# In the first pair of heads, the first head's two small query groups are transposed on TensorE and not through DRAM

## The chip, the cores and the metric

The kernel runs on one core of a Trainium2 chip. The metric is the time of one execution on the device in microseconds (us), smaller being better. Five engines work side by side, each through its own queue in order: PE (TensorE: matmuls, and PEld for its weight loads), DVE (VectorE), ACT (ScalarE), POOL (GpSimd) and SP, which here issues every DMA.

## The reference, cut to what matters

One decoder layer on x (1024 x 1024, fp32): RMSNorm, an input projection into eight parts, three mixers (causal pooling, stick-breaking attention, attention into a memory), each gated, then an output projection and the residual. The change is in the stick-breaking attention, 8 heads of 64 channels:

```python
z = einsum('bqhd,bkhd->bhqk', qb, kb) * Dh**-0.5      # a block of 128 queries, keys up to its end
mask = s_idx[None, :] < t_idx[:, None]
log_1m_beta = where(mask, log_sigmoid(-z), 0.0)
cum = cumsum(log_1m_beta, axis=-1)
log_a = log_sigmoid(z) + cum[..., -1:] - cum
a = where(mask, exp(log_a), 0.0)
out = einsum('bhqk,bkhd->bqhd', a, vb)
```

## The kernel before, in words

**The attention.** The 8 heads are worked off in four pairs. The queries of a head form four groups j = 0 to 3 of 256 queries (two blocks of 128), which look at 256, 512, 768 and 1024 keys. So there are 32 groups in the order (pair, j, head); in the first pair group 0 is head 0 with j = 0, group 1 is head 1 with j = 0, group 2 is head 0 with j = 1, and so on to group 7. Each group is cut into chunks of 256 keys, j + 1 of them: chunk 0 belongs to group 0, chunk 1 to group 1, chunks 2 and 3 to group 2, 4 and 5 to group 3, 6 to 8 to group 4, 9 to 11 to group 5. A group's last chunk is 384 columns wide (its upper triangle is left out), every other one 512.

For each block, `qk` (L743) multiplies queries with keys on PE (L754, tiles `z`), takes a sigmoid of -z on ACT into a scratch tile `be` (L760), and a scan on DVE turns it into running products (`scan`, L769). The result has queries on partitions and keys along the row, and the product with the values (`av`, L830, matmuls in `a_v` at L611) wants keys on partitions. Two ways lead there, and `by_dma` (L740) says which one a group takes:

- through DRAM: DVE transposes 32 x 32 squares (`turn`, L772), four DMAs per block write them to a DRAM tile `zd` so that the squares themselves change places (`store`, L780), and per chunk one or two DMAs bring them back to a tile `al` (`rd`, L801 to L807). ACT rounds that to `ah` (L826) and POOL subtracts to leave the low part in `al` (L827).
- on PE: `hl` (L810) calls `a_t` (L587), which transposes 128 x 128 blocks on PE into PSUM (L593, tiles `ta`), rounds them on ACT to `ah` (L597) and subtracts on DVE into `al` (L598).

Either way `a_v` multiplies first with `ah` and then with `al`. Before, the second head of each pair goes through DRAM whole, the first head only for j < 2.

**The order.** All engines' orders are written out by hand in this part. `sb_slots` gives each chunk e a slot: in slot e the kernel issues the reads of chunk e + 3, does `hl` of chunk e + 1 and `av` of chunk e. The `qk` steps of the groups are spread over slots ahead of their chunks (L857 to L863): the pair of groups n, n + 1 must be done 6 slots ahead of chunk first[n] when group n goes through DRAM, 3 slots ahead when it doesn't. Slots with nothing in them take no time. `weave` (L216) puts the slots between the steps of the input projection that PE does anyhow (the `fill`: units `u_q`, `u_k`, `u_g` of 16 steps, three 512-column matmuls to a step), giving each slot that has steps the same share of PE's planned time:

```python
span = sum(s.pe for s in main) + sum(c for c, _ in fill[: len(fill) - keep])
total = sum(s.occ + s.pe for s in main)
...
at_ = max([span * gone / total] + [ready.get(k, 0.0) for k in s.needs])
while n < len(fill) and now < at_:
```

Work that follows later is queued with `soon(us, fn)`: it is written into its engine's order once so many planned us have gone by (the scan 1.0 after its `qk`, a `turn` 1.1 + 0.0022 L and a `store` 3.4 + 0.0038 L for a row of L keys). The first pair's slots run from -12 to 8 beside 56 fill steps: the whole of `u_q` and `u_k` of the second pair, the gate unit `u_g` of the second pair, and half of that of the third. The first step of a unit also issues the load of the next unit's raw weights (`load`, L152, into the one buffer `wr`), and its steps 7, 9, 11 and 13 round quarters of them on ACT (L277) and subtract on POOL (L278).

**Buffers.** `be` tiles come from a ring of four, and every fifth and sixth from `Y0` and `Y1`; `al` is a ring of four, `ah` of two, the PSUM tiles `z` and `tr` (for `ta`) of two each.

Of the kernel before, what the change touches and what calls it, by code (L numbers as in the profile page):

```python
# [27 lines left out]
def layer_kernel(  # L28
# [707 lines left out]
    def sb_slots():  # L736
        groups = [(p, j, h) for p in range(4) for j in range(NT // 2) for h in range(2)]
        chunks = [(n, b) for n, (p, j, h) in enumerate(groups) for b in range(j + 1)]
        first = [chunks.index((n, 0)) for n in range(len(groups))]
        by_dma = [h == 1 or j < 2 for _, j, h in groups]  # L740
        be, zd, wt, acc, stored, n_be = {}, {}, {}, {}, [], [0]

        def qk(n, i, c):  # L743
# [418 lines left out]
    def y_load():  # L1162
# [13 lines left out]
        )  # L1176
    )
    attn = sb_slots()
    weave(attn[0], fill_0)
    weave(attn[1], fill_1)  # L1180
# [227 lines left out]
```

## Time and profile before

| | us |
|---|---|
| median of 3 runs (lowest to highest) | 518.09 (516.09 to 518.65) |
| the profiled execution | 514.25 |
| its span, first to last instruction | 512.5 |
| PE busy / DVE busy in the span | 491.7 / 405.4 |
| first `z` of the first pair | 136.23 |
| first `z` of the second pair | 197.06 |

All times of rows are us from the start of that span. The profiled execution took 1.75 us more than its span, and it is 3.84 us below the median of the runs.

### The profile page before, as it was taken

The numbers are of one execution on the slowest core, as the hardware profiler recorded it, in microseconds if no ns is written. First come the engines' busy times: TensorE is split into PE (matmuls) and PEld (weight loads), VectorE is DVE, ScalarE is ACT, GpSimd is POOL, SyncE is SP. The second block draws the span as 40 slices with busy tenths as digits, with TensorE's granted clock in tenths as the row PEclk, the third lists the DMA queues.
The fourth block names the chain that finished last, engine by engine and source line by source line (L and its number), as shares of the span: only waits on it lengthen the run. The fifth ranks groups of instructions, "written<-read, shape, count | busy, mean of one in ns | idle before, by whom it ended". The sixth has DMA issues, their size and how long they took to land.

```text
span 512.5 us, 8041 instructions
## 1 busy us (share of the span) xinstructions
PE 491.7 (96%) x2508; PEld 409.6 (80%) x2508; DVE 405.4 (79%) x618; ACT 297.3 (58%) x672; POOL 261.1 (51%) x254
## 2 busy tenths in 40 slices
PE   7999999999999799999999999999979989999997
PEld 6778888887888578888888888888758768888886
DVE  4787777777479578699988859878899659999954
ACT  7978757678455465566766666664754439362400
POOL 4480345265133336267662865765758870044990
PEclk9999999999999999999999999999999989999999
DMA  8911111532636944579876786768654822504023
GB/s 297 361 41 42 41 43 41 115 84 70 148 72 125 197 110 105 134 148 229 148 153 159 142 191 143 146 152 172 141 105 158 287 86 82 175 31 159 8 104 143
DMA packets 174979, 67.73 MB, mean 132 GB/s; under 512 B 125894, under 2 KB 164056, under 8 KB 174936
## 3 DMA queue, kind: packets, MB, share of 16 engines
q1 hardware_dynamic: 174936, 67.21, 52.6%
q8 instruction: 20, 0.33, 0.3%
q14 instruction: 23, 0.19, 0.1%
HBM read 43.59 MB, written 19.40 MB: 123 GB/s over the span
## 4 chain that ended last, share of the span: by engine, by line
PE 67%; DVE 10%; DMA 7%; ACT 5%; issue 4%; SPq 3%; POOL 3%; DVEq 0%; ACTq 0%; POOLq 0%
PE u_q L254 6%; PE av L611 6%; PE u_k L254 4%; DMA al<-zd 4%; PE u_v L254 4%; PE z L754 3%; DVE be L769 3%; PE u_q L251 3%; PE oS L1288 3%; PE oS L1290 3%; PE oS L1289 3%; SPq L780 3%; PE u_pg L254 2%; PE u_g L254 2%; PE u_k L251 2%
## 5 line engine op out<-in xcount | busy, mean ns | idle before, releaser
L769 DVE TENSOR_TENSOR_SCAN be<-be,later 128x128 f32<-128x128 f32 (+3 forms) x64 | 103.3, 1615 | 23.3 <-ACT be L760 22.7
L827 POOL TENSOR_TENSOR al<-al,ah 128x512 fp32r<-128x512 f32 (+1 forms) x52 | 76.4, 1474 | 37.0 <-ACT ah L826 32.7
L760 ACT ACTIVATE be<-z 128x128 f32<-128x128 f32 (+3 forms) x96 | 46.8, 489 | 33.9 <-PE z L754 25.8
L826 ACT ACTIVATE ah<-al 128x512 fp32r<-128x512 f32 (+1 forms) x52 | 30.1, 580 | 23.2 <-DMA al<-zd 21.2
L611 PE MATMUL av<-al,V_v 128*128 128x256 f32 (+1 forms) x160 | 32.8, 287 | 10.4 <-POOL al L827 6.0
L611 PEld LDWEIGHTS av<-ah,V_v 128*128 128x128 f32 x160 | 29.3, 188 | 9.7 <-ACT ah L826 2.9
L611 PEld LDWEIGHTS av<-al,V_v 128*128 128x128 f32 x160 | 24.1, 188 | 12.9 <-POOL al L827 7.5
L772 DVE STREAM_TRANSPOSE be<-be 128x128 f32<-128x128 f32 (+7 forms) x48 | 32.8, 685 | 1.1
L611 PE MATMUL av<-ah,V_v 128*128 128x256 f32 (+1 forms) x160 | 30.4, 271 | 2.1 <-ACT ah L826 2.1
L703 POOL TENSOR_SCALAR pe_m<-pe_m,nb_m 128x256 f32<-128x256 f32 x16 | 16.8, 1049 | 28.2 <-DVE nb_m L700 24.4
L597 ACT ACTIVATE ah<-ta 128x512 fp32r<-128x512 f32 (+1 forms) x28 | 15.9, 567 | 19.5 <-PE ta L593 17.8
L251 PE MATMUL u_v<-hh,wh_v 128*128 128x512 f32 x64 | 26.4, 412 | 0.0
L630 ACT ACTIVATE avt<-av,ve_v 64x128 f32<-64x128 f32 x64 | 19.8, 357 | 11.3 <-PE av L611 10.5
L251 PE MATMUL u_g<-hh,wh_g 128*128 128x512 f32 x64 | 26.2, 410 | 0.0
L1288 PE MATMUL oS<-bs,hh 128*128 128x512 f32 (+1 forms) x68 | 25.9, 381 | 0.0
L251 PE MATMUL u_k<-hh,wh_k 128*128 128x512 f32 x64 | 25.9, 404 | 0.0
L692 ACT ACTIVATE pe_m<-z_m,nb_m,qsc 128x256 f32<-128x256 f32 x32 | 17.8, 561 | 13.9 <-DVE nb_m L688 12.9
L1290 PE MATMUL oS<-bs,hl 128*128 128x512 f32 (+1 forms) x68 | 25.8, 379 | 0.0
L1289 PE MATMUL oS<-bs,hh 128*128 128x512 f32 (+1 forms) x68 | 25.6, 376 | 0.0
L754 PE MATMUL z<-KA_k,qa_q 128*128 128x512 f32 (+3 forms) x96 | 25.3, 348 | 0.0
L254 PE MATMUL u_v<-hl,wh_v 128*128 128x512 f32 x64 | 25.3, 395 | 0.0
L254 PE MATMUL u_g<-hl,wh_g 128*128 128x512 f32 x64 | 25.3, 395 | 0.0
(323 smaller groups left out, 1547.6 us busy)
## 6 DMA issues: line engine op xcount, KB each, us to landing
al<-zd SPq DMA_DIRECT2D x28, 256.0 KB, 3.1
x<-in_x_dram SPq DMA_DIRECT2D x8, 512.0 KB, 6.4
al<-zd SPq DMA_DIRECT2D x24, 128.0 KB, 3.2
wr_q<-in_w_in_dram SPq DMA_DIRECT2D x4, 512.0 KB, 5.3
wr_k<-in_w_in_dram SPq DMA_DIRECT2D x4, 512.0 KB, 5.0
wr_v<-in_w_in_dram SPq DMA_DIRECT2D x4, 512.0 KB, 3.8
KA_k<-KA_k SPq DMA_DIRECT2D x8, 256.0 KB, 4.8
KB_k<-KB_k SPq DMA_DIRECT2D x8, 256.0 KB, 3.9
```

The lines of the kernel that those rows point to most:

```text
L251: nc.tensor.matmul(pt[:], wh[:, kc], hh[k][:, c], start=(k == 0), stop=False)
L254: nc.tensor.matmul(pt[:], w[:, kc], h[k][:, c], start=False, stop=(k == KD - 1 and n == 1))
L611: nc.tensor.matmul(av[:, 256 - bw : 256], vs[n], part[:, o : o + bw], start=(first and part is ah and n == 0), stop=(last and part is al a ...
L754: nc.tensor.matmul(zp[:, 0:w], q[h][:, tcol], k[h][:, m, s0 : s0 + w], start=(m == 0), stop=(m == 1))
L760: nc.scalar.activation(t[:, s0 : s0 + w], zp[:, 0:w], AF.Sigmoid, scale=-(HD**-0.5))
L769: nc.vector.tensor_tensor_scan(t[:, rev], t[:, rev], mask, 1.0, op0=ALU.mult, op1=ALU.max)
L772: nc.vector.transpose(t[:, 0:L], t[:, 0:L])
L826: nc.scalar.activation(hi[:, 0:w], f(lo[:, 0:w]), AF.Copy)
L827: nc.gpsimd.tensor_tensor(lo[:, 0:w], f(lo[:, 0:w]), f(hi[:, 0:w]), op=ALU.subtract)
L1288: nc.tensor.matmul(bk[:, c], xh[:, tcol], wh[:, c], start=(n == 0), stop=False)
L1289: nc.tensor.matmul(bk[:, c], xh[:, tcol], wl[:, c], start=False, stop=False)
L1290: nc.tensor.matmul(bk[:, c], xl[:, tcol], wh[:, c], start=False, stop=(n == 3))
```

## The change

One line: which groups go through DRAM. In the first pair the groups 0 and 2 (first head, j = 0 and 1; chunks 0, 2 and 3) now take the way over PE. The slots and the interleaving follow from `by_dma`, so they move too.

```diff
-        by_dma = [h == 1 or j < 2 for _, j, h in groups]
+        by_dma = [h == 1 or (j < 2 and p > 0) for p, j, h in groups]
```

## Rows read from the trace of the kernel before

**Rows 1.** The page's first part: busy us, share of span, instructions.
```profile
PE 491.7 (96%) x2508; PEld 409.6 (80%) x2508; DVE 405.4 (79%) x618; ACT 297.3 (58%) x672; POOL 261.1 (51%) x254
```

**Rows 2.** Busy by stretch: length, PE, PEld, DVE, ACT, POOL, granted clock, DMA share.
```profile
134.00:170.00 36.00, 36.00 (x170) 29.63 (x169) 25.96 (x34) 16.89 (x38) 9.95 (x11) 1.00 0.54 109
170.00:196.00 26.00, 21.60 (x110) 17.37 (x109) 17.73 (x19) 14.20 (x31) 9.92 (x9) 1.00 0.71 161
196.00:230.00 34.00, 34.00 (x186) 29.06 (x185) 27.88 (x36) 20.05 (x46) 18.43 (x16) 1.00 0.54 114
```

**Rows 3.** Waits between 170 and 196: us in total, times, longest.
```profile
PEld av L611 <- POOL al L827: 3.1, 4, 1.1
...
PEld av L611 <- ACT ah L826: 2.1, 1, 2.1
...
PEld av L611 <- DVE al L598: 0.7, 2, 0.4
```

**Rows 4.** Timeline of ACT, 171 to 178 (start, us, idle before and releaser).
```profile
171.53 0.63 ACT L826 ACTIVATE ah<-al 128x512 fp32r<-128x512 f32 x1 [3.24 <-DMA al<-zd]
...
172.68 0.59 ACT L413 ACTIVATE g_g<-u_g 128x512 f32<-128x512 f32 x1
175.99 0.42 ACT L277 ACTIVATE wh_g<-wr_g 128x256 fp32r<-128x256 f32 x1 [2.71 <-DMA wr_g<-in_w_in_dram]
...
177.39 0.51 ACT L826 ACTIVATE ah<-al 128x384 fp32r<-128x384 f32 x1
```

**Rows 5.** Timeline of SP's queue, 149 to 178.
```profile
149.31 9.59 SPq L780 DMA_DIRECT2D zd<-be  x16
...
168.90 0.85 SPq L152 DMA_DIRECT2D wr_g<-in_w_in_dram  x1
...
172.34 5.31 SPq L780 DMA_DIRECT2D zd<-be  x4
177.76 0.47 SPq L801 DMA_DIRECT2D al<-zd  x1
```

**Rows 6.** Timeline of PE: the first product of chunk 2 to the second pair's first z.
```profile
172.52 0.40 PE L611 MATMUL av<-ah,V_v 128*128 128x256 f32 x2
173.58 0.51 PE L611 MATMUL av<-al,V_v 128*128 128x256 f32 x2 [0.66 <-POOL al L827]
...
177.95 0.45 PE L611 MATMUL av<-ah,V_v 128*128 128x256 f32 x2 [1.65 <-ACT ah L826]
179.30 0.45 PE L611 MATMUL av<-al,V_v 128*128 128x256 f32 x2 [0.90 <-POOL al L827]
...
197.06 0.33 PE L754 MATMUL z<-KB_k,qb_q 128*128 128x128 f32 x2
```

**Rows 7.** The chain that ended last: a chunk's transposes, and issue steps beside them.
```profile
202.78 0.44 PE ta L593 x4
...
203.44 0.47 PE u_q L254 x2
...
211.89 0.33 PE ta L593 x3
...
212.92 0.47 PE z L754 x2
213.38 0.47 PE av L611 x4
```

**Rows 8.** Groups by line: busy us, mean ns of one.
```profile
L593 PE MATMUL ta<-ident,be 128*128 128x128 f32 x104 | 15.9, 272 | 0.0
```

**Rows 9.** DVE's groups by shape, 134 to 200: busy us, mean ns, idle before.
```profile
L769 DVE TENSOR_TENSOR_SCAN be<-be,later 128x896 f32<-128x896 f32 x2 | 4.7, 2352 | 4.1 <-ACT be L760 4.1
L769 DVE TENSOR_TENSOR_SCAN be<-be,later 128x768 f32<-128x768 f32 x2 | 4.1, 2036 | 3.0 <-ACT be L760 3.0
L769 DVE TENSOR_TENSOR_SCAN be<-be,later 128x640 f32<-128x640 f32 x2 | 3.4, 1682 | 1.0 <-ACT be L760 1.0
...
L772 DVE STREAM_TRANSPOSE be<-be 128x512 f32<-128x512 f32 x2 | 1.4, 712 | 0.1
...
L598 DVE TENSOR_TENSOR al<-ta,ah 128x512 fp32r<-128x512 f32 x2 | 1.4, 680 | 0.0
```

## The prediction

> **What bounds the kernel now.** I read the page's first part, then busy time by stretch, then for the one stretch that loses time the waits, ACT's and SP's timelines and PE's own. PE is busy 96% of the span [rows 1], so most of the kernel is PE's issue order, and time is to be had only where PE stands still. Around the change that is one place: from 134 to 170 and from 196 to 230 PE is busy throughout, between 170 and 196 it is busy 21.60 of 26.00 us [rows 2]. The waits say on what: seven waits of the value products `av`, 3.1 us on POOL's `al`, 2.1 us on ACT's `ah`, 0.7 us on DVE's `al`, 5.9 us together [rows 3].
>
> The busy time hides part of this, since matmul records overlap; the issue order doesn't. From the first product of chunk 2 (172.52) to the second pair's first `z` (197.06) pass 24.54 us [rows 6]. The work in between, counted from the code: 15 fill steps of three matmuls, a matmul 0.235 us (two take 0.47), 10.6 us; six pairs of 512-column `z` at 0.47 and two of 384 at three quarters of that, 3.5 us; seven `av` at 0.47, 3.3 us; 11 transposes at 0.11, 1.2 us [rows 7]. That is 18.6 us, so 5.9 us are lost, the same figure.
>
> Why: chunk 2 comes late through DRAM (ACT waits 3.24 us for its DMA), then ACT, in order, waits 2.71 us for the raw weights of the next gate unit until 175.99, and chunk 3's rounding stands behind that until 177.39 [rows 4]. PE starts chunk 3's products at 177.95 and 179.30, and chunk 2's second product waited too [rows 6]. Behind this is SP: from 149.31 on it issues without a pause, 0.60 us a store (16 in 9.59 us), so the load of the weights gets out at 168.90 only, and chunk 4's read at 177.76 [rows 5].
>
> **The change part by part.** *Removed.* Groups 0 and 2 are four blocks: 16 stores and the reads of chunks 0, 2 and 3 (2 + 1 + 2), 21 DMAs, at some 0.5 to 0.6 us of SP each [rows 5] 10 to 12 us of SP's queue, from the very stretch where it is behind. Four DVE `turn`s: the 512-key one is 0.71 [rows 9], the shorter ones less, about 2 us. Three POOL subtractions. ACT's three roundings stay, from PSUM in place of SBUF.
>
> *Added to PE.* 3 + 4 + 3 = 10 transposes. A chunk of four takes 0.44 us of the issue order, one of three 0.33 [rows 7]: 0.44 + 2 x 0.33 = **1.1 us**, and PE has no slack here, so all of it counts. The record of one transpose is 0.272 us [rows 8], but records overlap as those of the matmuls do. As bounds: 1.1 by the issue order, 2.7 by the record. I take 1.1.
>
> The page "TensorE: Matmul & The Clock Gate" of the Trainium skill (Part 4: PE-mode transpose) gives some 275 ns for a 128 x 128 transpose within a kernel, and says that such work does not hold the clock up as matmuls do. The trace has the 272 ns as a record, issues one each 0.11 us, and shows a granted clock of 1.00 with eleven transposes among the matmuls [rows 2]; by the page's figure the sum would lose 2.75 us in place of 1.1.
>
> *Added to DVE.* Three subtractions for chunks 0, 2 and 3, 0.68 for 512 columns [rows 9] and less for 384: 1.7 us, about what the `turn`s give back.
>
> *Moved.* The pairs of groups (0, 1) and (2, 3) need a lead of 3 slots, no longer 6. Following L857 to L863: group 1 goes from slots -12, -11 to -12, -10; group 0 from -9, -8 to -7, -5; group 3 from -6 to -3; group 2 from -5 to -2; group 5 from -4..-2 to -1, 0; group 4 from 0, 1 to 1, 2; groups 7 and 6 stay at 3 to 8. Slots with steps fall from 19 to 16, and the planned work goes from 50.24 to 51.56 us, so a slot gets 3.22 planned us and not 2.64. From the second pair's first slot on both orders are the same, so what is won or lost by then reaches the end unless a later stage has a limit of its own; PE is busy all of 196 to 230 [rows 2], which speaks against that. The read of chunk 1 is now issued in slot -2 past fewer stores, the reads of 4 and 5 stay in slots 1 and 2.
>
> *What the removed waits turn into.* I turn planned into real time from the first `z` at 136.23 with 1.07 (worked out without its waits, the second pair's first `z` stands at 197.06 - 5.9 = 191.2 for 51.5 planned). Chunks 2 and 3, which carried four of the seven waits, depend on no DMA any more. The load of the gate weights is written at 25.24, real 163; ahead of it on SP stand only group 3's stores (its turns end by about 158) and one pair of copies, so it issues some 6 us earlier than 168.90. Even at 7.1 us to land (168.90 to 175.99) it is there by 170, and ACT asks for it at 33.24, real 172. Should it be late all the same, chunk 3's rounding now stands ahead of it on ACT. Chunk 4's read (25.89) issues by 164 to 165, where it was 177.76, for products at 176.8.
>
> *What is late next: DVE.* Groups 3, 2, 5 and 4 now scan one behind the other. Queue from group 5's first scan, ready about 160.6: scan 1.68, turn 0.85, the two low parts of `k` 1.4, scan 2.04, output of group 0 0.85, turn 0.98, then chunk 2's `al` 0.68: 169.1. PE wants it at 31.77 planned, 170.2 + 0.2. Then scan 1.68, output 0.85, chunk 3's `al` 0.53: 172.2, wanted at 173.9. Then scan 2.04, gate 0.66, scan 2.35, output 0.85, turn 1.10, chunk 6's `al` 0.68: 179.9, wanted at 184.5; so on to chunk 8 at about 188.8, wanted at 190.4 [rows 9]. Everything fits, with 1.3 to 1.7 us to spare at the tightest places. One scan that comes 1 us late upstream eats most of that, so I set down **1.0 us** of new waits: 0 if the queue goes as worked out, 2.4 if it runs one long scan behind throughout. The new transposes wait on scans too: group 2's are done by about 160, and PE wants them at 164.8 (26.65 planned); behind a late one would stand all of PE.
>
> *At nothing.* Group 5's first scratch tile is group 0's, freed by transposes that PE issues one or two fill steps after the sigmoid that wants it, so ACT stands still for about 1 us; ACT is busy 16.89 of 36 us there [rows 2] and PE has its second `z` bank. If that cover went, 1 us.
>
> **Sum**: -5.9 + 1.1 + 1.0 = **-3.8 us**. The profiled execution of 514.25 becomes 510.45; it lies 3.84 below the median of 518.09, so as a median **514.3 us**. Bounds of this case: -5.9 + 1.1 = -4.8 at best (512.5 with 0.8 for what I can't see), -5.9 + 1.1 + 2.4 = -2.4 at worst.
>
> **The rivals.** *DVE takes over in part.* For: DVE has 4 us and more of idle ahead of its scans in the stretch of before [rows 9], which goes, and the chunks on PE wait for DVE subtractions that stand behind scans; two of the seven waits are of that kind already [rows 3]. Against: the queue above. If DVE runs 4 us behind, two scans, less the 1.3 to spare, new waits are 2.4 to 4.8: between -2.4 and 0, 515.7 to 518.1.
>
> *The transposes cost their records.* 2.7 for 1.1: -2.2, 515.9. Against it, the issue order [rows 7].
>
> *PE has no time to give: the wait moves.* The products wait as long on other things (the reads of chunks 4 and 5, group 5's stores), and PE has 1.1 us more to do: +1.1, 519.2. For: waits in a chain often move on. Against: SP's backlog, which all of them share, goes.
>
> The Trainium skill, page "Perfetto Trace Analysis", section "Identifying the Most-Contended Engine", says to relieve the engine with the highest occupancy first; here that is PE, and the change loads it, which by that rule costs 1.1 us. That rule is read over the whole kernel; in this stretch PE waits 5.9 us for others.
>
> *Slower.* One place: DVE's queue between 160 and 190. If it runs more than 8.7 us behind (the 5.9 - 1.1 that the change wins, 2.6 for half a per cent, and 1.3 to spare), each further us is one of loss; at 10 us behind, +3.9, 522. For: four groups' scans stand together. Against: all their scans, turns and subtractions are in the sum above, and a standing PE lets DVE catch up.
>
> **How the numbers follow.** The forecast (-4.8 to -2.4, with its own range 512.5 to 515.7) gets 0.64, DVE in part 0.20, the records 0.04, the moved wait 0.07, slower 0.05. Half a per cent is 2.6 us, about what a measurement of this kernel can tell from no change. Faster by more: the forecast and a little of DVE in part, 0.67. Within: the rest of that, records and moved wait, 0.27. Slower: 0.06, with a little for what I don't see. The range, forecast and DVE in part together (0.84): 512.5 to 518.3.
>
> **What would show it.** In the profile after: 21 transposes, not 11, ahead of the second pair's first `z`; no `zd` store for groups 0 and 2; the load of the third pair's gate weights issued near 163 with no ACT wait on it; no `av` wait on ACT or POOL between 165 and 190; the second pair's first `z` at about 193. If that `z` stands where it did, the wait has moved: the waits of `av` on DVE's `al` then tell the second case, on POOL's `al` the fourth. If it stands at 193 and the whole is no shorter, a later stage took it back.

## The result, and the profile after

The changed kernel took a median of 510.9 us (510.09 to 512.9, 4 runs) beside 518.28 (516.09 to 518.65, 4 runs) for the kernel before: ratio 0.9891, 95% interval 0.9847 to 0.9935 (the ratio as recorded; the quotient of the two medians is 0.9858). A second comparison of the same two kernels gave 510.39 beside 514.09, ratio 0.993 (0.9901 to 0.9958). The forecast, 514.3 beside 518.09, is a ratio of 0.9927 and lies in both intervals. The time of 510.9 by itself lies below the low end of the range, 512.5; as a ratio of 518.09 the first comparison gives 512.4, at that end, the second 514.5. Before the second I had expected 0.988 to 0.992 if all of what is won around the change reaches the end, and 0.993 to 0.996 if a part is given back: 0.993 stands at the edge of the latter, and its interval takes in both. The profiled execution took 511.55 us (span 509.8), 2.70 less than that of before.

The page's first part, busy us, to be read beside [rows 1]: ten PE instructions more (the transposes), three POOL subtractions fewer, one DVE instruction fewer (four `turn`s against three subtractions).

```profile
PE 491.2 (96%) x2518; PEld 410.3 (80%) x2518; DVE 405.4 (80%) x617; ACT 297.1 (58%) x672; POOL 259.2 (51%) x251
```

Busy time by stretch, columns as in [rows 2]:

```profile
134.00:170.00 36.00, 36.00 (x177) 29.94 (x176) 24.15 (x32) 18.30 (x43) 10.25 (x10) 1.00 0.45 104
170.00:196.00 26.00, 26.00 (x139) 22.10 (x138) 23.02 (x25) 15.68 (x36) 12.74 (x12) 1.00 0.63 134
196.00:230.00 34.00, 33.77 (x183) 28.51 (x182) 28.28 (x35) 19.87 (x46) 13.96 (x13) 1.00 0.58 124
```

Between 170 and 196 PE was busy 21.60 us and is now busy 26.00; the view of waits lists none of PE between 134 and 196 where [rows 3] had seven. DVE rose from 17.73 to 23.02 in the same 26 us (25 instructions where it was 19): PE gets further there, and DVE's work for later chunks comes with it.

PE's timeline after: the first `z` of the first pair, the three groups of new transposes, the products of chunks 2, 3 and 4, and the first `z` of the second pair. None has a wait in brackets; [rows 6] had them at chunk 2 and twice at chunk 3.

```profile
136.74 0.34 PE L754 MATMUL z<-KB_k,qb_q 128*128 128x128 f32 x2
...
159.07 0.49 PE L593 MATMUL ta<-ident,be 128*128 128x128 f32 x3
...
165.38 0.62 PE L593 MATMUL ta<-ident,be 128*128 128x128 f32 x4
...
169.10 0.49 PE L593 MATMUL ta<-ident,be 128*128 128x128 f32 x3
...
170.59 0.40 PE L611 MATMUL av<-ah,V_v 128*128 128x256 f32 x2
...
173.98 0.34 PE L611 MATMUL av<-ah,V_v 128*128 128x256 f32 x2
...
176.99 0.40 PE L611 MATMUL av<-ah,V_v 128*128 128x256 f32 x2
...
192.51 0.33 PE L754 MATMUL z<-KB_k,qb_q 128*128 128x128 f32 x2
```

From first `z` to first `z` pass 55.77 us (192.51 - 136.74); before it was 60.83 (197.06 - 136.23). This length, which I call the stretch, is 5.06 us shorter. It is the measure of the experiments, because it repeats within 0.01 us (55.78 in a second trace of the changed kernel, 55.76 in two kernels that differ from it only in later pairs; of the kernel before there is one trace) while the whole varies by microseconds for a reason told further down.

SP's queue after, beside [rows 5]: the load of the gate weights leaves at 163.68 (before 168.90), chunk 4's read at 164.38 (before 177.76). ACT, beside [rows 4], starts on those weights at 173.69 with no wait on them.

```profile
163.68 0.52 SPq L152 DMA_DIRECT2D wr_g<-in_w_in_dram  x1
164.38 1.21 SPq L801 DMA_DIRECT2D al<-zd  x1
```

```profile
173.69 0.42 ACT L277 ACTIVATE wh_g<-wr_g 128x256 fp32r<-128x256 f32 x1
```

DVE's subtractions of chunks 2, 3, 6 and 8. They end at 169.89, 172.81, 180.18 and 188.95; the prediction had put 169.1, 172.2, 179.9 and 188.8:

```profile
169.25 0.64 DVE L598 TENSOR_TENSOR al<-ta,ah 128x512 fp32r<-128x512 f32 x1
172.25 0.56 DVE L598 TENSOR_TENSOR al<-ta,ah 128x384 fp32r<-128x384 f32 x1
...
179.49 0.69 DVE L598 TENSOR_TENSOR al<-ta,ah 128x512 fp32r<-128x512 f32 x1
...
188.42 0.53 DVE L598 TENSOR_TENSOR al<-ta,ah 128x384 fp32r<-128x384 f32 x1
```

### The profile page after: what moved, and what is told of

The parts are those of the page before. It is cut to its first block, busy times and chain, and to the rows that moved or that the text cites. A ratio compares the mean times of both kernels' runs of the same rounds, so it can differ in the third digit from the quotient of the medians.

```text
span 509.8 us, 8004 instructions
## 1 busy us (share of the span) xinstructions
PE 491.2 (96%) x2518; PEld 410.3 (80%) x2518; DVE 405.4 (80%) x617; ACT 297.1 (58%) x672; POOL 259.2 (51%) x251
## 4 chain that ended last, share of the span: by engine, by line
PE 77%; DVE 6%; DMA 5%; ACT 5%; POOL 2%; issue 2%; SPq 2%; ACTq 0%; DVEq 0%; POOLq 0%
PE av L611 7%; PE u_q L254 6%; PE z L754 6%; PE u_k L254 5%; PE u_g L254 4%; DMA al<-zd 4%; PE u_v L254 4%; PE u_q L251 3%; PE u_pg L254 3%; PE oS L1288 3%; PE oS L1290 3%; PE oS L1289 3%; PE u_k L251 3%; PE ta L593 2%; PE u_g L251 2%; PE oA L1290 2%
## 5 line engine op out<-in xcount | busy, mean ns | idle before, releaser
L769 DVE TENSOR_TENSOR_SCAN be<-be,later 128x128 f32<-128x128 f32 (+3 forms) x64 | 102.0, 1596 | 21.9 <-ACT be L760 21.2
L827 POOL TENSOR_TENSOR al<-al,ah 128x512 fp32r<-128x512 f32 (+1 forms) x49 | 74.7, 1527 | 35.0 <-ACT ah L826 31.4
L826 ACT ACTIVATE ah<-al 128x512 fp32r<-128x512 f32 (+1 forms) x49 | 28.5, 581 | 15.9 <-DMA al<-zd 13.5
L772 DVE STREAM_TRANSPOSE be<-be 128x128 f32<-128x128 f32 (+7 forms) x44 | 30.7, 700 | 1.0
L597 ACT ACTIVATE ah<-ta 128x512 fp32r<-128x512 f32 (+1 forms) x31 | 17.4, 563 | 21.8 <-PE ta L593 20.2
L254 PE MATMUL u_k<-hl,wh_k 128*128 128x512 f32 x64 | 25.3, 396 | 0.0
```

The source lines that it names most:

```text
L254: nc.tensor.matmul(pt[:], w[:, kc], h[k][:, c], start=False, stop=(k == KD - 1 and n == 1))
L769: nc.vector.tensor_tensor_scan(t[:, rev], t[:, rev], mask, 1.0, op0=ALU.mult, op1=ALU.max)
L772: nc.vector.transpose(t[:, 0:L], t[:, 0:L])
L826: nc.scalar.activation(hi[:, 0:w], f(lo[:, 0:w]), AF.Copy)
L827: nc.gpsimd.tensor_tensor(lo[:, 0:w], f(lo[:, 0:w]), f(hi[:, 0:w]), op=ALU.subtract)
```

## The experiments

Twelve runs. In the table, the stretch is as above; "waits" are PE's waits in it, summed over the lines of the view of waits; "second pair" is first `z` to first `z` of the pair after; "rest" is from the second pair's first `z` to the end of the span. The ratio is that of each kernel to the kernel before in its own comparison; where a kernel was timed once, that time stands.

| kernel | stretch | waits | second pair | rest | ratio (95%), or one time |
|---|---|---|---|---|---|
| before | 60.83 | 5.9 | 60.61 | 315.4 | 1 |
| changed | 55.77 | 0 | 61.48 | 317.3 | 0.9891 (0.9847 to 0.9935) |
| changed, again | 55.78 | 0 | 61.20 | 317.2 | 0.9930 (0.9901 to 0.9958) |
| slots of before | 55.79 | 0 | 61.20 | 315.3 | 0.9918 (0.9889 to 0.9947) |
| group 2 alone | 55.44 | 0 | 61.71 | 316.5 | 0.9960 (0.9936 to 0.9985) |
| group 2 alone, again | 55.43 | 0 | 61.93 | 318.0 | 0.9933 (0.9904 to 0.9961) |
| group 0 alone | 61.35 | 6.4 | 61.21 | 320.4 | 1.0054 (1.0030 to 1.0077) |
| 16 stores put back | 55.76 | 0 | 61.21 | 316.8 | 0.9937 (0.9904 to 0.9969) |
| transposes tripled | 57.96 | 0 | 61.64 | 319.3 | 1.0002 (0.9975 to 1.0030) |
| before, weights by POOL | 59.92 | 5.3 | 61.44 | 318.4 | 516.35 |
| before, group 2's stores by ACT | 57.50 | 2.8 | 61.22 | 319.5 | 514.99 |
| before, two queues | 57.88 | 3.0 | 61.18 | (see there) | 0.9938 (0.9905 to 0.9971) |
| second pair too | 55.76 | 0 | 62.88 | 322.4 | 0.9963 (0.9932 to 0.9995) |
| all pairs | 55.76 | 0 | 62.88 | 322.2 | 1.0020 (0.9995 to 1.0044) |

**Do the moved slots matter?** The way over PE, but with the slots of before; chunk 0 is transposed in slot -6 so that its scratch tiles come free in time.

```diff
-            c0, c1 = c1, first[n] - (6 if by_dma[n] else 3)
+            c0, c1 = c1, first[n] - (6 if by_dma[n] or n < 4 else 3)
...
-            if 0 <= e + 1 < len(chunks):
+            if e == -6:
+                b = [(0.44, lambda: hl(0))]
+            elif 1 <= e + 1 < len(chunks):
```

> Way over PE as after, but the slots of before (a lead of 6 for both pairs of groups; chunk 0 is turned in slot -6 so that its scratch tiles come free). Measured by the first pair's stretch, from its first z to the second pair's first z: 60.83 us before, 55.77 after. Theory, the way over PE is the gain and the moved slots are not: 55 to 56.5 and no av wait in the stretch over 0.5 us in all. Rival, the later slots (SP's stores spread out, a slot of 3.2 planned us) give it: 57.5 to 60.

The stretch is 55.79 against 55.77: the move of the slots carries nothing of the gain in it.

**Which group pays?** Group 2 alone over PE, in two runs, and group 0 alone (in the slots of before).

```diff
-        by_dma = [h == 1 or j < 2 for _, j, h in groups]
+        by_dma = [h == 1 or (j < 2 and (p > 0 or j == 0)) for p, j, h in groups]
```

> Only group 2 (chunks 2 and 3) goes over PE, group 0 through DRAM with its lead of 6. Seven transposes, so 0.77 us of PE; 10 DMAs stay on SP that the change removed, 11 go. Theory A, the gain is that chunks 2 and 3 wait for no DMA: stretch 55.3 to 56.3, as good as the whole change. Theory B, the gain is SP's shorter queue for the weights and the later chunks: half of the 5.1 us, 57.5 to 59.

> Only group 0 (chunk 0) goes over PE, with the slots of before; chunks 2 and 3 go through DRAM. Three transposes, 0.33 us of PE; 10 of the 21 DMAs gone from SP ahead of the load of the gate weights. Theory A (chunks 2 and 3 must leave DRAM): their waits stay, stretch 58.5 to 61. Theory B (SP's queue was behind; 10 DMAs of 0.55 us give 5.5 us): the load goes out near 163, chunk 3's wait of 2.9 us and those of chunks 4 and 5 (1.1) go, 55.5 to 57.

Group 2 alone gives the whole gain and 0.33 to 0.34 us more, the three transposes of group 0 that it leaves out. Group 0 alone gives nothing: 61.35, 0.52 longer than before, a little above the 58.5 to 61 of the theory that chunks 2 and 3 must leave DRAM and far from the 55.5 to 57 of the other. PE still waits seven times in the stretch, 6.4 us where it was 5.9 (us in total, times, longest):

```profile
PEld av L611 <- POOL al L827: 2.7, 3, 1.1
PEld av L611 <- ACT ah L826: 1.9, 2, 0.9
PEld av L611 <- DVE al L598: 1.8, 2, 1.5
```

Why does SP not get ahead when group 0's eight stores and two reads are gone? Its queue in this kernel:

```profile
147.31 0.39 SPq L152 DMA_DIRECT2D wr_g<-in_w_in_dram  x1
152.82 8.73 SPq L780 DMA_DIRECT2D zd<-be  x16
...
168.31 1.03 SPq L152 DMA_DIRECT2D wr_g<-in_w_in_dram  x1
```

SP stands idle from 147.70 to 152.82, since the next stores wait for DVE's `turn`s (the longest such wait is 5.0 us), and then issues the 16 of groups 3 and 2. They end at 161.55; in the kernel before, group 2's last ones ended at 162.01. The first pair starts 0.44 us earlier in this trace too, so that is no gain at all. The load of the weights leaves at 168.31, 0.59 earlier than before, 0.15 counted from the first `z`. The DMAs of group 0 had filled time in which SP would have waited.

The second run of group 2 alone was to tell whether the first one's 0.996 meant that group 0 matters elsewhere.

> The kernel with only group 2 (chunks 2 and 3) over PE once more, in more rounds. It has three transposes fewer than the changed kernel, 0.33 us, and its stretch in the trace was 55.44 against 55.77. First theory (the whole gain is group 2, group 0 only costs its transposes): ratio 0.988 to 0.993, the changed kernel's or a little below. Rival (group 0's stores also matter somewhere else in the kernel): the 0.996 of its first timing comes again.

0.9933 is the changed kernel's ratio within the interval; the 0.996 did not come again.

**Is it SP's queue that was relieved?** The changed kernel with the 16 stores of groups 0 and 2 issued all the same, to a DRAM tile that nobody reads.

```diff
+            def spare_store():
+                for a in range(4):
...
+                    nc.sync.dma_start(zd[n][0:L, o : o + 32]..., t[q, 0:L]...)
...
+                if n in (0, 2):
+                    soon(3.4 + 3.8e-3 * L, spare_store)
```

> The kernel after, and the 16 stores of groups 0 and 2 are put back on SP with their times and sizes; nobody reads what they write (the output is unchanged). Theory A (path): chunks 0, 2 and 3 stay free of DMA, so the stretch stays at 55.8 to 57 although SP is behind again. Theory B (SP's queue and DMA traffic): the gate weights, chunk 4 and chunk 5 come late again, 58 to 60.

The stores are back on SP (L789), and with them the load of the weights is late again, 167.13:

```profile
162.48 4.55 SPq L789 DMA_DIRECT2D zd<-be  x8
167.13 0.46 SPq L152 DMA_DIRECT2D wr_g<-in_w_in_dram  x1
167.63 0.59 SPq L812 DMA_DIRECT2D al<-zd  x1
```

and the stretch is 55.76, with no wait of PE. So these 16 stores and the late weights cost nothing once chunks 2 and 3 do not come through DRAM. The run does not put back all of SP's delay: chunk 4's read (the last line) leaves 3.25 us later than in the changed kernel but 10 us earlier than before (177.76), since in the moved slots it stands ahead of group 5's stores. A chunk 4 as late as before was not tried with chunks 2 and 3 on PE.

**What does one transpose cost?** The changed kernel with each of the ten new transposes done three times, 20 more.

```diff
-                nc.tensor.transpose(tp[:, o : o + P], src, ident[:])
+                for _ in range(3 if name in ("0", "2", "3") else 1):
+                    nc.tensor.transpose(tp[:, o : o + P], src, ident[:])
```

> The kernel after with each of the ten new transposes done three times (20 more; the output is unchanged). By the issue order of 0.11 us each the stretch grows by 2.2 us, from 55.77 to 58.0; by the record of 0.272 us each it grows by 5.4 us, to 61.2. No other engine gets work.

```profile
158.50 1.14 PE L594 MATMUL ta<-ident,be 128*128 128x128 f32 x9
...
194.13 0.33 PE L755 MATMUL z<-KB_k,qb_q 128*128 128x128 f32 x2
```

The second pair's first `z` stands at 194.13, 57.96 after the first pair's (136.17). 57.96 - 55.77 = 2.19 us for 20, 0.11 each: the issue interval of [rows 7], not the record of 0.272 [rows 8]. The whole became 4.3 us longer than the changed kernel of the same comparison (514.65 against 510.39); the other 2 us are in the rest, most of them at the end of the kernel (below).

**What did the late weights cost before?** The kernel before, with that one load issued from POOL's queue.

```diff
-        nc.sync.dma_start(raw[:], src)
+        (nc.gpsimd if name == "g2" else nc.sync).dma_start(raw[:], src)
```

> The kernel before, but the raw weights of the third pair's gate are loaded from POOL's queue, so their load stands behind nothing on SP. If the late weights, ahead of chunk 3's rounding on ACT, make that chunk late (the prediction's reading), the stretch falls from 60.83 to 58 to 59 and the 2.7 us wait of ACT goes. If chunk 2's and 3's own way through DRAM is late anyway (as group 0 alone over PE suggests), it stays at 60 or more.

The load leaves at 162.19, ACT's 2.71 us of waiting on it are gone, and the stretch is 0.91 shorter, no more: 59.92, between the two expectations. Chunk 4's read still leaves at 176.86, and PE still waits 5.3 us.

The 0.91 is a balance and not the price of the late weights. PE's wait of 2.10 us for chunk 3's rounding is gone, but two waits came that the kernel before doesn't have: 0.94 us for a sigmoid (at 169.43) and 1.20 us for chunk 2's rounding (at 174.18). Behind both is ACT's rounding of chunk 1, which stands 2 us later, first before, then with the load on POOL's queue:

```profile
166.37 0.53 ACT L826 ACTIVATE ah<-al 128x384 fp32r<-128x384 f32 x1 [0.38 <-DMA al<-zd]
```

```profile
168.37 0.53 ACT L826 ACTIVATE ah<-al 128x384 fp32r<-128x384 f32 x1 [2.42 <-DMA al<-zd]
```

Its read was issued at the same time in both (162.11 and 162.04); what is new beside it is the load of 512 KB. That the load held the read up is read from these rows, and no run separates it.

**What did group 2's stores cost before?** The kernel before, with the eight stores of group 2 issued from ACT's queue.

```diff
-                    nc.sync.dma_start(
+                    (nc.scalar if n == 2 else nc.sync).dma_start(
```

> The kernel before, but the eight stores of group 2 are issued from ACT's queue; all traffic stays. If SP's queue makes chunks 2 and 3 late, they are stored and read some 4 us earlier, their waits go, and the stretch falls to 56.5 to 58.5 (ACT pays some 0.5 us a store out of its idle time). If the way through DRAM itself, or the traffic, makes them late, the waits stay and the stretch is 60 or more.

3.33 us of the 5.06 are won with no more transposes on PE than before. Chunks 2 and 3 (products at 172.51 and 175.19) wait for nothing now. Their reads leave 1.9 and 2.4 us earlier than before (166.33 and 167.40), not 4. The load of the weights leaves 2.0 us earlier as well (166.92), and ACT waits 0.25 us for it, so the 3.33 takes in part of what the late weights cost. What is left stands at the chunks behind:

```profile
PEld av L611 <- POOL al L827: 1.6, 2, 1.0
PEld av L611 <- DVE al L598: 0.8, 2, 0.4
PEld av L611 <- ACT ah L826: 0.4, 1, 0.4
```

```profile
169.94 4.57 SPq L780 DMA_DIRECT2D zd<-be  x4
174.62 0.46 SPq L801 DMA_DIRECT2D al<-zd  x1
```

Chunk 4's read stands behind four stores of group 5, which wait for their `turn`. The last run takes the reads of chunks 4 and 5 out from behind them as well.

```diff
+            q = nc.gpsimd if e in (4, 5) else nc.sync
...
-                nc.sync.dma_start(
+                q.dma_start(
```

> The kernel before with no change of way: group 2's eight stores issue from ACT's queue (as in the run before that did this alone, first pair's stretch 57.50, waits of av 2.8 us), and the reads of chunks 4 and 5 (three DMAs) from POOL's queue, where they don't stand behind group 5's stores on SP. First theory (what PE loses in this stretch is the order of DMA issues on SP alone): chunk 4's read issues near 165, not 174.62, the waits on ACT's ah and POOL's al for chunks 4 and 5 (about 1.7 us) go, 0.8 on DVE stays, the stretch becomes 55.3 to 56.0, as short as with transposes on PE, without the 1.1 us of them; ratio 0.990 to 0.994. Rival (the way through DRAM is slow in itself: landing, ACT's rounding and POOL's 1.27 us stand between a read and the product): the waits on POOL and ACT move to the chunks behind, the stretch stays at 57 to 58, ratio 0.995 to 1.000.

Its profiled execution was its longest (519.15, beside a median of 513.17), so I read only the stretch from it, in which the granted clock is 1.00 throughout. Chunk 4's read leaves at 168.47, 6.15 us earlier than in the run before though not near 165, and the products of chunks 4 and 5 come without a wait. But the stretch is 57.88, not the 55.3 to 56.0 of the first theory:

```profile
PEld av L611 <- DVE al L598: 1.9, 2, 1.5
PEld av L611 <- POOL al L828: 1.1, 1, 1.1
```

The 1.1 on POOL is chunk 3's, as the rival said of POOL though not of the chunk. POOL's timeline shows what stands ahead of its subtraction at 175.76, and DVE's which scan it delays:

```profile
172.06 1.94 POOL L278 TENSOR_TENSOR wl_g<-wr_g,wh_g 128x256 fp32r<-128x256 f32 x1 [0.21 <-ACT wh_g L277]
173.95 0.57 POOL L807 DMA_DIRECT2D al<-zd  x1
174.52 0.54 POOL L808 DMA_DIRECT2D al<-zd  x1
175.07 0.75 POOL L278 TENSOR_TENSOR wl_g<-wr_g,wh_g 128x256 fp32r<-128x256 f32 x1
175.76 1.00 POOL L828 TENSOR_TENSOR al<-al,ah 128x384 fp32r<-128x384 f32 x1
...
179.35 1.00 POOL L828 TENSOR_TENSOR al<-al,ah 128x384 fp32r<-128x384 f32 x1
```

```profile
176.39 5.84 DVE L769 TENSOR_TENSOR_SCAN be<-be,later 128x896 f32<-128x896 f32 x1 [1.41 <-ACT be L760]
```

The two reads that were put on POOL's queue take 1.1 us of it, and subtractions without a pause until 180.35 follow them. The scan beside it takes 5.84 us, where the other one of this kernel takes 1.98 (190.25), and ends 1.9 us after POOL's last subtraction. All of DVE's later work is behind it, chunk 7's `al` with a wait of 1.30 at 189.23. The Trainium skill ("SBUF — State Buffer", section "SBUF: two separate sides") says that a DVE operation with two inputs in SBUF and a GpSimd operation that reads SBUF lock each other out of a pair of ports for a whole instruction; the length of this scan agrees, and no run separates it. In the kernel before, the scan of this shape at 182.10 starts 0.44 us into a POOL subtraction of 1.28 and takes 2.72 us; the one at 192.85, with POOL idle, takes 1.98.

So SP's order is the larger part of the loss, but I did not find an order of the queues that gives back the last 2 us with the DRAM way kept; whether one exists stays open. The timed ratio, 0.9938, lies in the range of the first theory, where the stretch lies in that of the rival; it cannot be told from the changed kernel's.

**Does it pay in other pairs?** The same for the second pair as well, and for all four.

```diff
-        by_dma = [h == 1 or j < 2 for _, j, h in groups]
+        by_dma = [h == 1 or (j < 2 and p > 1) for p, j, h in groups]
```

> The small groups of the first head of the second pair go over PE as well (in the first pair as in the changed kernel). First theory (the way over PE pays only where the small groups' own chunks wait for the way through DRAM): in the second pair's stretch of the kernel before PE waits 1.1 us in all, only on DVE's al and not on DRAM, so nothing is won and ten transposes are paid. From the second pair's first z to the third's: before 60.61, changed kernel 61.2 to 61.5; expected 62.3 to 62.6. The first pair's stretch stays at 55.8. Rival (the way over PE is cheaper in general, since it relieves SP, POOL and the DMA engines): the second pair's stretch becomes shorter than 61.2, at best by the 1.1 of waits less the transposes, that is, not more than 61.2, and the whole no slower than the changed kernel's ratio of 0.989 to 0.993.

> The small groups of the first head go over PE in all four pairs. First theory: three times 1.1 us of transposes against the changed kernel and nothing won in pairs two and three; ratio against the kernel before about 0.997 (0.9965 to 1.000). In the last pair the waits of PE (4.1 us on POOL, 4.0 on DVE) belong to later groups and stay. Rival: the DMA queue and POOL, relieved in the last pair, give back the 4.1 us of waits on POOL there, and the ratio is 0.990 or below.

The second pair's stretch becomes 62.88 where it was 61.20 to 61.48 in the changed kernel, a little above the 62.3 to 62.6 that transposes alone would give: there is a new wait of 1.21 us on DVE as well. (The 1.1 us of waits that the first of these expectations gives the second pair before holds two waits of the first pair, at 191.83 and 195.33; in the second pair's own stretch stands one of 0.4 us.) PE's timeline, then DVE's ahead of it:

```profile
237.35 0.45 PE L611 MATMUL av<-al,V_v 128*128 128x256 f32 x2 [1.21 <-DVE al L598]
```

```profile
232.90 1.44 DVE L769 TENSOR_TENSOR_SCAN be<-be,later 128x640 f32<-128x640 f32 x1
...
235.30 0.68 DVE L344 TENSOR_TENSOR KA_k<-u_k,KA_k 64x512 fp32r<-64x512 f32 x1
...
236.74 0.56 DVE L598 TENSOR_TENSOR al<-ta,ah 128x384 fp32r<-128x384 f32 x1
```

The subtraction stands behind a scan, two gate steps and the two low parts of `k`: the very case that the prediction feared for the first pair. In all pairs the ratio is 1.002 (0.9995 to 1.0044), above the 0.9965 to 1.000 of the first theory by its middle: the waits on POOL fell as the rival said (after 196 from 5.3 in the changed kernel to 2.1), but others grew, at L983 on DVE from 1.0 to 3.5 us, and 3.2 us of `z` on ACT came new. No version beats the changed kernel by more than the intervals.

## Why the prediction came out, point by point

**The place and the sum of the waits: right.** All of the gain is in the 26 us that [rows 2] showed, and all seven waits went. Without waits and without transposes the stretch would be 55.77 - 1.10 = 54.67; before it was 60.83, so 6.16 us were lost there, for 5.9 predicted. One reading was wrong: chunks 2 and 3 carried three of the seven waits ([rows 6]), not four, though with 0.87, 2.10 and 1.05 us (PEld's waits, which [rows 3] sums) they were 4.0 of the 5.9. The other four, of 0.3 to 0.6 us, stood at chunks 4, 5, 7 and 8.

**The transposes: right.** 1.10 us for ten, measured by tripling. The rival by records is dead; so is the sum with the some 275 ns of the Trainium skill ("TensorE: Matmul & The Clock Gate", Part 4: PE-mode transpose): that figure is the record's length (272 ns here), and 20 of them would have been 5.5 us where 2.19 were measured.

**New waits on DVE: the term that was mis-sized.** I had set 1.0 us; 0 came. The queue itself went in the order worked out, 0.2 to 0.8 us later at the four subtractions, which is 0.4 earlier to 0.3 later counted from the first `z`, 0.51 us later in this trace. The factor of 1.07 that turned planned into real time set the old kernel's time without waits beside the new kernel's plan; beside the old plan of 50.24 it would have been 1.09, and 55.77 for 51.56 is 1.08. The allowance was not foolish: in the second pair the same change brings 1.21 us of just this wait.

**At nothing: right.** ACT does stand still for 0.98 us, until 159.38, for the transposes that free a scratch tile, and PE doesn't wait for it.

**The sum** was therefore -3.8 for the stretch, and -5.06 was measured, more than the -4.8 that was set as best. Of the whole, 2.7 us are left in the profiled execution. From the first pair's first `z` on, the gain is 5.06 at the second pair's, 4.19 at the third's, 4.46 at the fourth's and 3.2 at the end of the span (372.9 or 373.1 against 376.3). Part of it is the second pair's stretch, 0.6 to 0.9 longer than in the one trace of before; PE waits 1.7 us in it, before 0.4. There ACT waits 1.56 us for the raw weights `wr_v` (before 0.53): they land at 227.73, only 3.5 us earlier, when the rest is 4.6 earlier. But kernels whose first pair gained less have 61.2 to 61.4 there too, so this was read, not shown. The end of the span is told below. By these traces, that the forecast of the whole fell so near is in part luck: 1.0 us of waits that did not come and some 2 us of gain that did not last took each other away. The timed comparisons can't tell: 0.9891 is 5.7 us of 518, 0.993 is 3.6, and 5.06 (a ratio of 0.9902) lies in both intervals.

**What bounded it: right about SP, wrong about how.** The prediction named SP's late issue, the load of the weights at 168.90, and 21 DMAs of relief. The runs split this:

- the load of the weights moved to another queue won 0.91 us, with new waits of 2.1 us in that balance, so the price of the late weights alone is not known; they cost nothing once chunks 2 and 3 no longer come through DRAM (16 stores back: load at 167.13, stretch 55.76);
- group 0's half of the relief was worth nothing: SP would have waited for DVE's `turn`s in that time;
- group 2's eight stores on SP were worth 3.33 us in one trace, with the 2 us by which the weights and the reads behind them came earlier; the rest went only with the whole way, which takes its turns, reads and POOL subtractions along.

So what counted were the waits of two chunks and of the ones queued behind them on SP. The step "10 to 12 us of SP's queue" counted instructions of the queue and not which of them anything late stood behind.

**The rivals.** The moved wait and the slow DVE queue did not come in the first pair. Waits on DVE do come elsewhere: of 1.5 us with two queues changed and of 1.21 us in the second pair.

## What to carry to other kernels

Trade a DMA round trip for work on the busiest engine only for those pieces whose own consumer waits in the trace: of two groups changed together here one gave 5.4 us net and the other cost its 0.33 us, and the same edit in a pair without such waits cost 1.4 us and more. And try the queue first: group 2's stores on another engine's queue gave 3.3 us of it with no more work on the busiest engine. When a queue is behind, ask of each DMA what stands behind it and whether the queue would have been idle in its place; the sum of their issue times is only a ceiling. Measure an edit by a stretch between two fixed instructions when the whole varies for other reasons.

## What the runs showed that I had not expected

The end of the kernel makes the whole vary by some 4 us between kernels that run the same instructions there: from the fourth pair's first `z` to the end of the span pass 188.5 us with the slots of before and 192.7 with group 0 alone. In the four traces that I compare (before, changed, group 0 alone, transposes tripled), PE has two waits of 2.3 to 2.8 us there, one on DVE and, some 32 us on, one on POOL. One thing that differs is whether the granted clock falls behind each. The waits before and in the run with group 0 alone:

```profile
380.71 0.45 PE L611 MATMUL av<-al,V_v 128*128 128x256 f32 x2 [2.58 <-DVE al L598]
...
412.41 0.44 PE L611 MATMUL av<-al,V_v 128*128 128x256 f32 x2 [2.58 <-POOL al L827]
```

```profile
382.99 0.45 PE L611 MATMUL av<-al,V_v 128*128 128x256 f32 x2 [2.58 <-DVE al L598]
...
416.06 0.69 PE L611 MATMUL av<-al,V_v 128*128 128x256 f32 x2 [2.77 <-POOL al L827]
```

Busy time around them, the third figure from the end being the granted clock; before:

```profile
380.00:385.00 5.00, 4.29 (x22) 3.62 (x23) 4.80 (x7) 2.89 (x7) 2.67 (x2) 1.00 0.21 33
...
415.00:420.00 5.00, 5.00 (x19) 3.96 (x18) 1.77 (x3) 0.00 (x0) 4.32 (x5) 0.81 0.00 0
```

the changed kernel:

```profile
380.00:385.00 5.00, 5.00 (x21) 4.13 (x20) 4.87 (x5) 1.62 (x4) 4.83 (x3) 0.77 0.25 74
...
415.00:420.00 5.00, 5.00 (x22) 3.72 (x21) 3.33 (x5) 2.17 (x5) 2.92 (x4) 1.00 0.00 0
```

group 0 alone:

```profile
385.00:390.00 5.00, 5.00 (x22) 4.20 (x20) 4.87 (x5) 1.38 (x4) 5.00 (x4) 0.70 0.32 94
...
415.00:420.00 5.00, 3.94 (x10) 3.24 (x11) 2.30 (x4) 1.65 (x5) 5.00 (x5) 0.53 0.26 94
```

The clock falls to its lower level for a part of the slice once in the first two kernels, after the second wait before and after the first one in the changed kernel, and twice with group 0 alone. The rest is 315.4, 317.3 and 320.4 us. The kernel with tripled transposes falls twice too (0.50 in 380 to 385, 0.81 and 0.84 in 410 to 420) and has 319.3. That more falls go with more time is read from these traces, and it is not the whole: before and changed have one fall each and yet 188.6 and 189.9 us from the fourth pair's first `z` on, and the first trace of group 2 alone, with a granted clock of 1.00 in every slice from 360 to 440, has 188.7. Why nearly equal waits let the clock fall in one kernel and not in another was not tried and stays open. It may be how 0.5 us lost in the first pair became 2.8 us of the whole with group 0 alone.
